# Pads that move TensorE's operands in SBUF, and another order of the first loads and splits

## The chip, the cores and the metric

The kernel runs on one core of one Trainium2 chip. The metric is device time in microseconds of one execution; the time of the kernel before is the median of three runs.

## The reference, cut

One sequence of 256 tokens with 1024 channels goes through two layers of a first block and one layer of a second block, all in fp32. Weights are used once for all 256 tokens, so most of the work is reading some 290 MB of weights and multiplying them with a small activation matrix.

```python
def first_block(x, ...):                      # two layers l
    h = _rmsnorm(x, norm_mix[l])
    p = h @ w_in[l]                           # 1024 x 3328, split over four mixers:
    branches = (rwkv7, stick_breaking, retention, conformer_conv)
    merged = sum(sigmoid(h @ w_gate[l, i]) * (branches[i] @ w_branch[l, i]) for i in range(4))
    x = x + merged @ w_out[l]
    h = _rmsnorm(x, norm_ffn[l])
    if l % 2 == 0: x = x + (silu(h @ ffn_w1) * (h @ ffn_w3)) @ ffn_w2      # width 2816
    else:          x = x + moe(h)             # top 2 of 8 SwiGLU experts, width 1408
def second_block(x, ...):                     # one layer
    proj = rms_norm(x) @ w_in                 # NSA attention, RG-LRU, two gates
    x = x + (sigmoid(ga) * (y_a @ w_proj_a) + sigmoid(gb) * (y_b @ w_proj_b)) @ w_out
```

## The kernel before, in words

**Products in three parts.** Every weight matrix is streamed from HBM in pieces of up to 128 x 2048 fp32 (tile `raw`, 1 MB, a DMA on SP's queue, `wload_` line 299). `wsplit_` cuts each half of a piece in a high part `wh` (ScalarE cast, line 266) and a rest `wl` (VectorE subtraction, line 267), both fp32r, 128 x 1024. Activations are split likewise, into `hh` and `hl` for the normed input, `uh`/`ul` inside the dense FFN, `bh`/`bl` for a mixer's branch, `mh`/`ml` for the merged sum, `xg` for the tokens gathered for an expert, `mu` for an expert's inner activations. A product is then three fp32r matmuls, all issued from line 131: in `dense`,

```python
if kind == "T":
    ps = ((h[:, kk, off:off + n], ah), (h[:, kk, off:off + n], al), (o[:, kk, off:off + n], ah))
else:
    x0, x1 = ah[:, j * P:(j + 1) * P], al[:, j * P:(j + 1) * P]
    ps = ((x0, h[:, kk, off:off + n]), (x0, o[:, kk, off:off + n]), (x1, h[:, kk, off:off + n]))
```

Kind "T" (nearly all) holds 128 columns of a weight stationary and streams 256 tokens of the activation. The other kinds hold the activation stationary and stream 384 or 512 columns of a weight: all w1, w3 and w2 products of the experts, and some projections ("R").

**Places in SBUF.** A tile's byte offset in each partition comes from the order in which pools and tiles are made. Pool `wp` has three slots each for `wh`, `wl` and `raw`. During the dense FFN and the experts, two more split slots stand in the pools `ffn` and `moe` (`spare`), and the slots are taken in turn. Tags `acth` and `actl` of pool `acts` (its tiles are `hh`/`hl`, later `mh`/`ml` of the second block and `hr` of the experts) lie right behind `wp`.

**Order.** A stage's work is written as generators, and a scheduler puts the instructions of each engine in order; `PLACES` pins some of TensorE's small products (recurrences, norms) between streamed ones. In one layer's mixers a chain of VectorE work (the RWKV-7 recurrence, near 110 to 180 us and 600 to 660 us) runs beside streamed products.

**The start** (`first_norm`, lines 1701 to 1731). SP loads constants, four pieces of `x` (tile `gth`), three pieces of `w_in`, the constants `c_mix` and small vectors (`pcvr`, `pcdr`); GpSimd's queue loads `wa`, `g2` and three vectors broadcast to all partitions (lines 530 to 538). ScalarE squares the four pieces of `x`, VectorE scales them by the inverse norm (line 1719), TensorE transposes them, and ScalarE (line 1728) and VectorE (line 1729) write `hh` and `hl` column block by column block. The list `behind` makes the first split wait for the scaled `x`. After the first 96 streamed products TensorE transposes the plain `x` again, for the residual `xT` (ScalarE copies, line 1742).

Of the kernel before, what the change touches and what calls it, by code (L numbers as in the profile page):

```python
# [18 lines left out]
P = 128  # L19
# [89 lines left out]
def build(tc, I, out, dbg=None, upto=99):  # L109
# [54 lines left out]
    ctile = {}  # L164
    late = {}

# [86 lines left out]
    def wsplit_(raw, k, n, perm):  # L253
        h, o = slot("split", [("wh", [P, 1024], F32R), ("wl", [P, 1024], F32R)])
        h = h[:, :k * n].rearrange("p (k n) -> p k n", n=n)
        o = o[:, :k * n].rearrange("p (k n) -> p k n", n=n)
        if perm:
            for g in range(2):
                src = raw[:, :, g * 256:(g + 1) * 256].rearrange("p k (b d) -> p k b d", d=64)
                hv = h.rearrange("p k (b g d) -> p k g b d", g=2, d=64)[:, :, g]  # L260
                ov = o.rearrange("p k (b g d) -> p k g b d", g=2, d=64)[:, :, g]
                for kk in range(k):
                    S.copy(out=hv[:, kk], in_=src[:, kk])
                    V.tensor_sub(out=ov[:, kk], in0=src[:, kk], in1=hv[:, kk])
        else:
            a = S.copy(out=h, in_=raw)  # L266
            i = V.tensor_sub(out=o, in0=raw, in1=h)  # L267
            if lead["n"]:
                lead["n"] -= 1
                if lead["late"] and not lead["n"]:  # L270
                    tc.add_manual_dep(i.ins, lead["late"].ins.name, nosync, reason="choice first")
                for x, y in zip((a, i), lead["ops"]):
                    tc.add_manual_dep(x.ins, y.ins.name, nosync, reason="activations first")
                for r in lead["hold"]:
                    tc.add_manual_dep(r.ins, i.ins.name, nosync, reason="first half first")
                lead["hold"] = ()
            if behind:
                tc.add_manual_dep(i.ins, behind.pop().ins.name, nosync, reason="norm first")
        return h, o

    def wload(src, k, n, rows=False, pinned=False):
        with tc.high_priority(offset=HP[1]):
            return wload_(src, k, n, rows, pinned)

    def wload_(src, k, n, rows, pinned):
# [9 lines left out]
        elif rows:  # L295
            for g in range(2):
                dma(out=r[g * 64:(g + 1) * 64], in_=src.rearrange("(g b p) n -> g p b n", g=2, p=64)[g])
        else:
# [194 lines left out]
    def bc_rows(mp, src, n, nm):  # L493
        t_ = mp.tile([P, n], F32, name=nm)
        nc.gpsimd.dma_start(out=t_, in_=bass.AP(tensor=src.tensor, offset=src.offset, ap=[[0, P], [1, n]]))
# [19 lines left out]
    def mix_layer(l):  # L515
        with ExitStack() as ls_:
# [10 lines left out]
            cload("c_mix", mp, nc.sync if l == 0 else nc.gpsimd)  # L527

            wa = mp.tile([P, 256], F32, name="wa")
            nc.gpsimd.dma_start(out=wa[0:64], in_=I["rw_w2"][l])  # L530
            nc.gpsimd.dma_start(out=wa[64:128], in_=I["rw_a2"][l])
            g2 = mp.tile([P, 256], F32, name="g2")
            nc.gpsimd.dma_start(out=g2, in_=I["rw_g2"][l])
            lnw = bc_rows(mp, I["rw_ln_w"][l], 256, "lnw")
            lnb = bc_rows(mp, I["rw_ln_b"][l], 256, "lnb")
            gn = bc_rows(mp, I["ret_gn"][l], 256, "gn")
            omu = mp.tile([P, 8], F32, name="omu")
            pts = [t2(f"pt{q}") for q in range(4)]
            for g in (1, 0):
# [8 lines left out]
                if g == 1:  # L548
                    if l == 0:
                        start_rest(mp)  # L550
                    V.tensor_scalar(omu, pc("mu"), -1.0, 1.0, op0=OP.mult, op1=OP.add)
                for c in range(4):
# [3 lines left out]
                    V.scalar_tensor_tensor(pt[:, b % 2, 1:], aps[c][:, :T - 1], pc("mu")[:, b:b + 1], pt[:, b % 2, 1:], op0=OP.mult, op1=OP.add)  # L556
            rT, kT, vT, pw = pts
# [757 lines left out]
    def lru(np_, W, hact):  # L1315
# [30 lines left out]
        V.scalar_tensor_tensor(ri, ri, 1.0, uc, op0=OP.add, op1=OP.mult)  # L1346
        a2 = np_.tile([P, 4, T], F32, name="la2", tag="lu")
# [96 lines left out]
    def moe(gain):  # L1444
        with ExitStack() as fs:
# [9 lines left out]

            xg = fp.tile([P, 2, KC, 2, P], F32R, name="xg")
# [5 lines left out]
            msq = [fp.tile([P, 2, T], F32, name="msq", tag="mth", bufs=3) for _ in range(3)]  # L1462
            mu = fp.tile([P, 2, 11, P], F32R, name="mu")
            hr = [ap_.tile([P, 2, D], F32R, name=f"hr{x}", tag=t_, bufs=1) for x, t_ in enumerate(("acth", "actl"))]
# [235 lines left out]
    def first_norm(mg, mp):  # L1700
# [3 lines left out]
        for j in range(2):  # L1704
            for a in range(2):
# [3 lines left out]
        start["pre"] = {1: [wload(I["w_in"][0, k * P:(k + 4) * P, 512:1024], 4, 512) for k in (0, 4)],  # L1709
                        0: [wload(I["w_in"][0, 0:512, 0:512], 4, 512)]}  # L1710
        xs = mp.tile([P, 2, 2], F32, name="xs")
        for j in range(2):
            for a in range(2):
                S.activation(out=h_rows[j][a], in_=x_rows[j][a], func=AF.Square, accum_out=xs[:, a, j:j + 1])
# [5 lines left out]
        behind.append(i)  # L1720
        start["gains"] = turned_columns(grows)
        hh, hl = ap_.tile([P, KC, T], F32R, name="hh", tag="acth", bufs=1), ap_.tile([P, KC, T], F32R, name="hl", tag="actl", bufs=1)
        for q in range(4):
            ps = rows_turned(h_rows, q)
            for c in range(2):
                k = 2 * q + c
                gk, pv = gains("nm", 0, 2)[:, k:k + 1], ps[:, c * T:(c + 1) * T]
                S.activation(out=hh[:, k], in_=pv, func=AF.Copy, scale=gk)  # L1728
                V.scalar_tensor_tensor(hl[:, k], pv, gk, hh[:, k], op0=OP.mult, op1=OP.subtract)
# [129 lines left out]
```

## Time and profile before

| | |
|---|---|
| time, median of 3 runs | 1436.39 us (1435.27 to 1437.26) |
| the profiled execution | 1438.56 us, of which the span is 1436.8 us |
| TensorE busy | 1382.1 us (96%), 10953 matmuls |
| VectorE busy | 1079.3 us (75%) |
| ScalarE busy | 804.5 us (56%) |
| mean granted clock of TensorE | 0.987 of full speed |
| HBM | 204 GB/s over the span |

A matmul's end is modelled in the profile, and successive matmuls overlap there. What one matmul adds to the time is the distance from its start to the next start, not its listed duration.

### The profile page before, as it was taken

How to read it: one execution, taken by the hardware profiler on the slowest of the kernel's cores; microseconds unless marked ns; L12 is line 12 of the kernel's file. 1: busy time of each engine (PE TensorE's matmuls, PEld its weight loads, DVE VectorE, ACT ScalarE, POOL GpSimd, SP SyncE). 2: the span in 40 equal slices, each digit the busy share in tenths (PEclk: the TensorE clock that was granted, in tenths of full speed). 3: DMA queues.
4: the chain of work that ended last, by engine and by line, in shares of the span. 5: the costliest groups of instructions: out<-in, count | busy, mean ns of one | idle time of the engine just before them, and what ended most of it. 6: DMA issues, size and time to landing. Idle time of an engine off the chain costs nothing. (4 is left out here: it accounts for less than half of the span.)

```text
span 1436.8 us, 26493 instructions
## 1 busy us (share of the span) xinstructions
PE 1382.1 (96%) x10953; PEld 1279.8 (89%) x10953; DVE 1079.3 (75%) x1569; ACT 804.5 (56%) x1126; POOL 54.7 (4%) x71
## 2 busy tenths in 40 slices
PE   5999999999999899998999799999999999899998
PEld 5999989999999889998999688888888888898997
DVE  4759966685655675797586799898898998767765
ACT  4643264564444454323544588788788777474643
POOL 1000010001000100002000000000000002010000
PEclk9999999999999999999999899999999999999999
DMA  7453134585566435422358599899799896734342
GB/s 242 150 193 118 32 120 162 187 296 189 194 131 209 137 128 169 147 87 75 132 183 293 187 365 355 296 361 356 282 371 358 287 339 207 262 120 131 107 134 101
DMA packets 137586, 294.24 MB, mean 205 GB/s; under 512 B 6949, under 2 KB 28845, under 8 KB 137200
## 3 DMA queue, kind: packets, MB, share of 16 engines
q1 hardware_dynamic: 133952, 282.48, 56.9%
q0 software_dynamic: 3424, 9.97, 2.9%
q8 instruction: 87, 1.43, 0.4%
q14 instruction: 43, 0.35, 0.1%
q10 hardware_dynamic: 80, 0.02, 0.0%
HBM read 289.82 MB, written 2.62 MB: 204 GB/s over the span
## 5 line engine op out<-in xcount | busy, mean ns | idle before, releaser
L267 DVE TENSOR_TENSOR wl<-raw,wh 128x1024 fp32r<-128x1024 f32 (+1 forms) x542 | 634.0, 1188 | 228.9 <-ACT wh L266 224.4
L266 ACT CAST wh<-raw 128x1024 fp32r<-128x1024 f32 (+1 forms) x542 | 549.1, 1022 | 444.5 <-PE mm L131 351.1
L131 PE MATMUL mm<-hh,wh 128*128 128x256 f32 x1376 | 396.7, 289 | 4.6 <-ACT hh L1728 3.0
L131 PE MATMUL mm<-hh,wl 128*128 128x256 f32 x1376 | 394.4, 287 | 5.0 <-DVE wl L267 2.5
L131 PE MATMUL mm<-hl,wh 128*128 128x256 f32 x1376 | 396.5, 288 | 0.0
L131 PEld LDWEIGHTS mm<-hh,wh 128*128 128x128 f32 x1376 | 267.3, 194 | 9.0 <-ACT hh L1728 3.4
L131 PEld LDWEIGHTS mm<-hh,wl 128*128 128x128 f32 x1376 | 267.1, 194 | 6.7 <-DVE wl L267 2.7
L131 PEld LDWEIGHTS mm<-hl,wh 128*128 128x128 f32 x1376 | 267.1, 194 | 3.5 <-issue 2.3
L131 PE MATMUL mm<-wh,xg 128*128 128x512 f32 (+1 forms) x768 | 231.5, 376 | 0.0
L131 PEld LDWEIGHTS mm<-wh,xg 128*128 128x128 f32 x768 | 142.7, 188 | 21.9
L131 PE MATMUL mm<-wl,xg 128*128 128x512 f32 (+1 forms) x384 | 143.9, 375 | 0.0
L131 PE MATMUL mx<-wh,mu 128*128 128x512 f32 x352 | 118.4, 398 | 0.0
L131 PEld LDWEIGHTS mm<-wl,xg 128*128 128x128 f32 x384 | 72.2, 188 | 11.2
L131 PEld LDWEIGHTS mx<-wh,mu 128*128 128x128 f32 x352 | 66.2, 188 | 13.5
L131 PE MATMUL mx<-wl,mu 128*128 128x512 f32 x176 | 69.3, 394 | 0.0
L955 DVE SCALAR_TENSOR_TENSOR cac<-cu,pcd,cac 128x256 f32<-128x256 f32 x120 | 52.9, 478 | 0.1
L131 PE MATMUL mx<-uh,wh 128*128 128x256 f32 x176 | 48.8, 280 | 1.4 <-ACT uh L218 1.4
L131 PE MATMUL mx<-ul,wh 128*128 128x256 f32 x176 | 49.1, 280 | 0.0
L131 PE MATMUL mx<-uh,wl 128*128 128x256 f32 x176 | 49.1, 279 | 0.0
L131 PE MATMUL mm<-nr,wh 128*128 128x256 f32 x192 | 38.3, 294 | 3.4 <-ACT nr L450 1.7
L131 PEld LDWEIGHTS mx<-wl,mu 128*128 128x128 f32 x176 | 33.1, 188 | 5.9
L131 PE MATMUL mm<-mh,wh 128*128 128x256 f32 x128 | 36.1, 282 | 0.0
(686 smaller groups left out, 2077.5 us busy)
## 6 DMA issues: line engine op xcount, KB each, us to landing
raw<-in_moe_w_dram SPq DMA_DIRECT2D x104, 1024.0 KB
raw<-in_w_in_dram SPq DMA_DIRECT2D x44, 1024.0 KB
raw<-in_ffn_w_dram SPq DMA_DIRECT2D x33, 1024.0 KB
raw<-in_w_gate_dram SPq DMA_DIRECT2D x32, 1024.0 KB
raw<-in_moe_w_dram SPq DMA_DIRECT2D x32, 768.0 KB
raw<-in_w_out_dram SPq DMA_DIRECT2D x12, 1024.0 KB
raw<-in_w_branch_dram SPq DMA_DIRECT2D x8, 1024.0 KB
raw<-in_moe_w_dram SPq DMA_DIRECT2D x8, 512.0 KB
```

The costliest lines, as they stand in the source:

```text
L131: i = getattr(nc.tensor, name)(*a, **k)
L266: a = S.copy(out=h, in_=raw)
L267: i = V.tensor_sub(out=o, in0=raw, in1=h)
L955: V.scalar_tensor_tensor(acc[:, b], cu[:, b, 2 + k:2 + k + T], dw[:, 2 * k + b:2 * k + b + 1], acc[:, b], op0=OP.mult, op1=OP.add)
```

## The change

**Pads.** A helper `pad(pool, n, name)` makes a tile of n bytes a partition that nothing uses, so that what follows in the pool stands n bytes further on. The byte offsets in the program as built, and what they leave when divided by 128 bytes:

| tile (pool) | before | after |
|---|---|---|
| `wh`, `wl` (wp) | 53184 to 73664 in steps of 4096: 64 | the same |
| `hh`, `hl` (acts) | 77760, 85952: 64 | 77824, 86016: 0 |
| `wh`, `wl` (ffn) | 120832 to 133120: 0 | 121344 to 133632: 0 |
| `uh`, `ul` (ffn) | 145408 to 159744: 0 | 145920 to 160256: 0 |
| `wh`, `wl` (moe) | 205888 to 218176: 64 | 207296 to 219584: 64 |
| `xg`, `mu` (moe) | 137216, 178432: 0 | 138176, 179648: 64 |
| `bh`, `bl`, `mh`, `ml` (mixers) | 64 in layer 0, 96 in layer 1 | 0, but for 16 of 768 products |

All offsets inside these tiles are multiples of 512 bytes. So of the streamed products of 256 columns, 3,768 with `hh` or `hl` and weights in `wp` go from (moving 64, stationary 64) to (0, 64); 360 with weights in the FFN's own two slots go from (64, 0) to (0, 0); 768 of the branches go to (0, 64). The experts' 1,680 wide products go from (64, 0) to (64, 64), and 192 products of 512 columns and 96 of 256 columns with `hh`, `hl`, `mh` or `ml` stationary go from (64, 64) to (64, 0). The 528 products of `uh` and `ul` stay (0, 64) or (0, 0).

**The start.** `x` is loaded and squared by channel halves; the two pieces of the first weight block are loaded in two halves each; the first three splits are tied to steps of the norm one after the other; `wa` moves from GpSimd's queue to SP's, behind the small vectors, and `c_mix`, `g2` and the broadcast vectors move to SP's queue behind the second weight block (layer 0 alone).

```diff
+    def pad(pool, n, nm):
+        pool.tile([P, n // 4], F32, name=nm, tag=nm, bufs=1)
...
             if behind:
-                tc.add_manual_dep(i.ins, behind.pop().ins.name, nosync, reason="norm first")
+                for x, y in zip((a, i), behind.pop(0)):
+                    tc.add_manual_dep(x.ins, y.ins.name, nosync, reason="norm first")
...
+        elif halves:
+            for x in range(2):
+                ks = slice(x * k // 2, (x + 1) * k // 2)
+                dma(out=r[:, ks], in_=src.rearrange("(k p) n -> p k n", p=P)[:, ks])
...
-            cload("c_mix", mp, nc.sync if l == 0 else nc.gpsimd)
             wa = mp.tile([P, 256], F32, name="wa")
-            nc.gpsimd.dma_start(out=wa[0:64], in_=I["rw_w2"][l])
-            nc.gpsimd.dma_start(out=wa[64:128], in_=I["rw_a2"][l])
             g2 = mp.tile([P, 256], F32, name="g2")
...
+            def first_vectors(eng):
+                eng.dma_start(out=wa[0:64], in_=I["rw_w2"][l])
+                eng.dma_start(out=wa[64:128], in_=I["rw_a2"][l])
+            def vectors(eng):
+                cload("c_mix", mp, eng)
+                eng.dma_start(out=g2, in_=I["rw_g2"][l])
+                return [bc_rows(mp, I[k][l], 256, nm, eng) for k, nm in (("rw_ln_w", "lnw"), ("rw_ln_b", "lnb"), ("ret_gn", "gn"))]
+            if l:
+                first_vectors(nc.gpsimd)
+                lnw, lnb, gn = vectors(nc.gpsimd)
...
+            pad(mp, (64, 32)[l], "padm")
...
                     if l == 0:
                         start_rest(mp)
+                        first_vectors(nc.sync)
...
+            if l == 0:
+                lnw, lnb, gn = vectors(nc.sync)
...
+        pad(np_, 64, "padl")
...
+            pad(fp, 448, "padx")
             xg = fp.tile([P, 2, KC, 2, P], F32R, name="xg")
...
+            pad(fp, 256, "padu")
             mu = fp.tile([P, 2, 11, P], F32R, name="mu")
+            pad(fp, 192, "pads")
...
-        for j in range(2):
-            for a in range(2):
+        for a in range(2):
+            for j in range(2):
                 nc.sync.dma_start(out=x_rows[j][a], in_=I["x"][0, j * P:(j + 1) * P, a * 512:(a + 1) * 512])
...
-        start["pre"] = {1: [wload(I["w_in"][0, k * P:(k + 4) * P, 512:1024], 4, 512) for k in (0, 4)],
+        start["pre"] = {1: [wload(I["w_in"][0, k * P:(k + 4) * P, 512:1024], 4, 512, halves=True) for k in (0, 4)],
                         0: [wload(I["w_in"][0, 0:512, 0:512], 4, 512)]}
...
-        behind.append(i)
+            if a == 0:
+                behind.append((sq, i))
         start["gains"] = turned_columns(grows)
+        pad(ap_, 64, "pada")
         hh, hl = ap_.tile([P, KC, T], F32R, name="hh", tag="acth", bufs=1), ap_.tile([P, KC, T], F32R, name="hl", tag="actl", bufs=1)
+        pad(ap_, 448, "padb")
...
+            if q in (0, 2):
+                behind.append((x, y))
```

ScalarE's queue at the start of the program, before the change: the squares of `x`, three casts of weights (`wh`), then the writing of `hh`.

```order
L1714 ACTIVATE gth,xs<-gth 128x512 x4
L266 CAST wh<-raw 128x1024 x3
L1728 ACTIVATE hh<-mx,pcg 128x256 x7
L266 CAST wh<-raw 128x1024
L1728 ACTIVATE hh<-mx,pcg 128x256
L266 CAST wh<-raw 128x1024 x2
L1742 COPY xT<-mx 128x512 x4
```

The same place after the change:

```order
L1738 ACTIVATE gth,xs<-gth 128x512 x4
L271 CAST wh<-raw 128x1024
L1755 ACTIVATE hh<-mx,pcg 128x256 x8
L1771 COPY xT<-mx 128x512
L271 CAST wh<-raw 128x1024 x3
L1771 COPY xT<-mx 128x512 x3
L271 CAST wh<-raw 128x1024 x3
```

Two casts have moved from ahead of `hh` to behind it, and a copy of the transposed `x` now stands ahead of the second cast. On TensorE the sixteen transposes for that copy have moved from behind the first 96 streamed products to behind the first 24.

SP's queue, which issues most DMAs, at the start before the change:

```order
L169 DMA c_id<-in_c_id_dram 128x256
L1706 DMA gth<-in_x_dram 128x512 x4
L299 DMA raw<-in_w_in_dram 128x4x512 x3
L169 DMA c_mix<-in_c_mix_dram 128x2192
L198 DMA pcvr<-in_rw_mu_dram 16x128
...
L198 DMA pcdr<-in_conv_dw_dram 124x128
L299 DMA raw<-in_w_in_dram 128x4x512 x3
```

And after it:

```order
L1730 DMA gth<-in_x_dram 128x512 x4
L307 DMA raw<-in_w_in_dram 128x2x512 x2
L309 DMA raw<-in_w_in_dram 128x4x512
L307 DMA raw<-in_w_in_dram 128x2x512 x2
L203 DMA pcvr<-in_rw_mu_dram 16x128
...
L542 DMA wa<-in_rw_w_dram 64x256
L543 DMA wa<-in_rw_a_dram 64x256
L309 DMA raw<-in_w_in_dram 128x4x512
L174 DMA c_mix<-in_c_mix_dram 128x2192
L547 DMA g_166<-in_rw_g_dram 128x256
```

The 1.1 MB of `c_mix` has moved from ahead of the small vectors to behind the fourth piece of weights, and `wa`, `g2` and the three broadcast vectors, which stood on GpSimd's queue, now stand here.

## Rows read from the trace of the kernel before

**Rows 1.** The page, busy time of each engine and its share of the span.

```profile
PE 1382.1 (96%) x10953; PEld 1279.8 (89%) x10953; DVE 1079.3 (75%) x1569; ACT 804.5 (56%) x1126; POOL 54.7 (4%) x71
```

**Rows 2.** Waits of the whole run: who for whom, us in total, times, longest.

```profile
ACT wh L266 <- PE mm L131: 351.1, 270, 12.7
...
PE mx L131 <- DVE g L1537: 8.4, 1, 8.4
```

**Rows 3.** TensorE's groups by shape, whole run: count, busy us, mean ns of one.

```profile
L131 PE MATMUL mm<-hh,wh 128*128 128x256 f32 x1376 | 396.7, 289 | 4.6 <-ACT hh L1728 3.0 <-ACT hh L218 1.6
...
L131 PE MATMUL mm<-wh,xg 128*128 128x512 f32 x512 | 164.1, 395 | 0.0
L131 PE MATMUL mx<-wh,mu 128*128 128x512 f32 x352 | 118.4, 398 | 0.0
L131 PE MATMUL mm<-wl,xg 128*128 128x512 f32 x256 | 100.8, 394 | 0.0
...
L131 PE MATMUL mm<-wh,xg 128*128 128x384 f32 x256 | 68.6, 339 | 0.0
L131 PE MATMUL mx<-ul,wh 128*128 128x256 f32 x176 | 49.1, 280 | 0.0
...
L131 PE MATMUL mm<-bh,wh 128*128 128x256 f32 x128 | 35.9, 284 | 0.0
```

**Rows 4.** The instructions in order of time, TensorE, 434 to 443 us: start, duration.

```profile
434.44 0.28 PE L131 MATMUL mm<-hh,wh 128*128 128x256 f32 x1
...
442.72 0.28 PE L131 MATMUL mm<-hh,wh 128*128 128x256 f32 x1
```

**Rows 5.** TensorE's groups by shape, 434.4 to 443.0 us.

```profile
L131 PE MATMUL mm<-hl,wh 128*128 128x256 f32 x25 | 7.1, 283 | 0.0
```

**Rows 6.** The same, 428.8 to 434.3 us.

```profile
L131 PE MATMUL mm<-hl,wh 128*128 128x256 f32 x17 | 4.8, 281 | 0.0
```

**Rows 7.** The same, 376.9 to 384.8 us.

```profile
L131 PE MATMUL mx<-ul,wh 128*128 128x256 f32 x24 | 6.6, 276 | 0.0
```

**Rows 8.** The same, 408.9 to 414.3 us.

```profile
L131 PE MATMUL mx<-uh,wh 128*128 128x256 f32 x16 | 4.5, 280 | 0.0
```

**Rows 9.** The same, 509.9 to 512.2 us.

```profile
L131 PE MATMUL mm<-nr,wh 128*128 128x256 f32 x14 | 2.5, 280 | 0.0
```

**Rows 10.** The same, 82.0 to 91.0 us.

```profile
L131 PE MATMUL mm<-wh,hl 128*128 128x512 f32 x14 | 5.4, 389 | 0.0
```

**Rows 11.** Stretch, its length; busy us of PE, PEld, DVE, ACT, POOL; PE clock; DMA share, GB/s.

```profile
120.00:170.00 50.00, 49.92 (x997) 46.58 (x996) 48.74 (x112) 13.99 (x21) 1.63 (x1) 1.00 0.27 87
...
940.00:980.00 40.00, 40.00 (x183) 33.14 (x182) 38.56 (x40) 32.80 (x37) 0.00 (x0) 1.00 1.02 374
```

**Rows 12.** TensorE in order of time, first 36 us: start, duration, idle before it.

```profile
12.63 3.86 PE L131 MATMUL mx<-c_id,gth 128*128 128x128 f32 x16 [6.05 <-DVE gth L1719]
19.54 0.79 PE L131 MATMUL mm<-hh,wh 128*128 128x256 f32 x2 [3.05 <-ACT hh L1728]
...
24.70 0.41 PE L131 MATMUL mm<-hh,wl 128*128 128x256 f32 x1
...
33.81 1.91 PE L131 MATMUL mx<-c_id,gth 128*128 128x128 f32 x16
```

**Rows 13.** ScalarE, the same stretch.

```profile
10.13 0.63 ACT L1714 ACTIVATE gth<-gth 128x512 f32<-128x512 f32 x1 [1.49 <-DMA gth<-in_x_dram]
...
15.34 1.99 ACT L266 CAST wh<-raw 128x1024 fp32r<-128x1024 f32 x2 [4.49 <-DMA raw<-in_w_in_dram]
...
19.02 2.66 ACT L1728 ACTIVATE hh<-mx,pcg 128x256 fp32r<-128x256 f32 x7
```

**Rows 14.** GpSimd, the same stretch: the DMAs that it issues.

```profile
1.25 0.72 POOL L530 DMA_DIRECT2D wa<-in_rw_w_dram  x1 [0.80 <-POOLq L1844]
...
4.12 0.56 POOL L495 DMA_DIRECT2D gn<-in_ret_gn_dram  x1
```

**Rows 15.** TensorE's groups by shape, 443.7 to 448.6 us.

```profile
L131 PE MATMUL mx<-uh,wh 128*128 128x256 f32 x15 | 4.2, 283 | 0.0
```

More of the change, by code (lines that the diff above doesn't have):

```diff
@@ L277, in wsplit_, with wload, wload_ @@
             if behind:
-                tc.add_manual_dep(i.ins, behind.pop().ins.name, nosync, reason="norm first")
+                for x, y in zip((a, i), behind.pop(0)):
+                    tc.add_manual_dep(x.ins, y.ins.name, nosync, reason="norm first")
         return h, o
-    def wload(src, k, n, rows=False, pinned=False):
+    def wload(src, k, n, rows=False, pinned=False, halves=False):
         with tc.high_priority(offset=HP[1]):
-            return wload_(src, k, n, rows, pinned)
-    def wload_(src, k, n, rows, pinned):
+            return wload_(src, k, n, rows, pinned, halves)
+    def wload_(src, k, n, rows, pinned, halves):
         raw, = slot("raw", [("raw", [P, 2048], F32)])
@@ L491, in ln_rows, with bc_rows @@
         V.tensor_tensor(out=y, in0=y, in1=r.unsqueeze(2).to_broadcast([P, 8, 64]), op=OP.mult)
-    def bc_rows(mp, src, n, nm):
+    def bc_rows(mp, src, n, nm, eng):
         t_ = mp.tile([P, n], F32, name=nm)
-        nc.gpsimd.dma_start(out=t_, in_=bass.AP(tensor=src.tensor, offset=src.offset, ap=[[0, P], [1, n]]))
+        eng.dma_start(out=t_, in_=bass.AP(tensor=src.tensor, offset=src.offset, ap=[[0, P], [1, n]]))
         return t_
@@ L525, in mix_layer @@
             hact = first_norm(mg, mp) if l == 0 else norm(gains("nm", l, 2), mg, "gth", 13)
-            cload("c_mix", mp, nc.sync if l == 0 else nc.gpsimd)
             wa = mp.tile([P, 256], F32, name="wa")
-            nc.gpsimd.dma_start(out=wa[0:64], in_=I["rw_w2"][l])
-            nc.gpsimd.dma_start(out=wa[64:128], in_=I["rw_a2"][l])
             g2 = mp.tile([P, 256], F32, name="g2")
[L533 to L536, printed above, removed]
+            def first_vectors(eng):
[8 more added lines that the diff above has]
+                lnw, lnb, gn = vectors(nc.gpsimd)
             omu = mp.tile([P, 8], F32, name="omu")
+            pad(mp, (64, 32)[l], "padm")
             pts = [t2(f"pt{q}") for q in range(4)]
@@ L1708, in first_norm @@
                                  ("ng", I["norm_gain_2"].rearrange("(a b) -> a b", b=P), 8)], "pcg", nc.scalar)
-        start["pre"] = {1: [wload(I["w_in"][0, k * P:(k + 4) * P, 512:1024], 4, 512) for k in (0, 4)],
+        start["pre"] = {1: [wload(I["w_in"][0, k * P:(k + 4) * P, 512:1024], 4, 512, halves=True) for k in (0, 4)],
                         0: [wload(I["w_in"][0, 0:512, 0:512], 4, 512)]}
         xs = mp.tile([P, 2, 2], F32, name="xs")
-        for j in range(2):
-            for a in range(2):
-                S.activation(out=h_rows[j][a], in_=x_rows[j][a], func=AF.Square, accum_out=xs[:, a, j:j + 1])
+        for a in range(2):
+            for j in range(2):
+                sq = S.activation(out=h_rows[j][a], in_=x_rows[j][a], func=AF.Square, accum_out=xs[:, a, j:j + 1])
         V.tensor_tensor(out=xs[:, 0], in0=xs[:, 0], in1=xs[:, 1], op=OP.add)
@@ L1727, in first_norm @@
                 gk, pv = gains("nm", 0, 2)[:, k:k + 1], ps[:, c * T:(c + 1) * T]
-                S.activation(out=hh[:, k], in_=pv, func=AF.Copy, scale=gk)
-                V.scalar_tensor_tensor(hl[:, k], pv, gk, hh[:, k], op0=OP.mult, op1=OP.subtract)
+                x = S.activation(out=hh[:, k], in_=pv, func=AF.Copy, scale=gk)
+                y = V.scalar_tensor_tensor(hl[:, k], pv, gk, hh[:, k], op0=OP.mult, op1=OP.subtract)
+            if q in (0, 2):
+                behind.append((x, y))
         start["x_rows"] = x_rows
```

## The prediction, made before the changed kernel had run

> **What bounds the kernel now.** I read the busy times first: TensorE is busy for 96% of the span, VectorE for 75% [rows 1]. Since a busy TensorE is not one at its peak, the list of waits comes next. ScalarE's casts of weights wait 351 us in 270 waits for matmuls to free a split slot, while TensorE's longest single wait is 8.4 us [rows 2]; casts, subtractions and DMAs all run ahead of TensorE. So the span is in the main the sum of the distances between matmul starts, and anything taken off those distances in the streamed stretches comes off the time, until VectorE gets in the way.
>
> How large is that distance? In a steady stretch of `hh`/`hl` products two rows 69 matmuls apart stand 8.28 us apart, 120 ns each [rows 4], and the same stretch lists 283 ns for one matmul [rows 5]. So a listed mean, less 163 ns, is the distance of steady matmuls; a mean over a whole run also holds some waits and cold stretches. Streaming 256 columns at 2.4 GHz, the level that the granted clock shows in nearly all of the span, is 106.7 ns of work: 13.3 ns are something else.
>
> The trace then shows that this rest depends on where the operands stand. Read by the moving and the stationary operand's offset modulo 128, at 256 columns:
> (64, 64): 283, so 120 ns [rows 5]; (64, 0), `hh` with weights in the FFN's slots: 281, so 118 [rows 6]; (0, 64), `uh`/`ul` with weights in `wp`: 276, so 113 [rows 7], but 280, so 117, in another such stretch [rows 8], and 280 for the (0, 64) tiles `nr` of a norm [rows 9].
> The whole-run mean for `ul` is 280 [rows 3]. With the 240 `uh`/`ul` products whose weights stand in the FFN's slots near 283, as at (64, 64), the 288 in `wp` come out near 277: most of these run at 113.
> At 512 columns the sign turns: (64, 64) has 389, so 226 [rows 10], the experts' (64, 0) have 394 to 398 [rows 3].
>
> So (0, 64) has two steady distances, 113 and 117 to 118. Which one a stretch falls in I can only read from what went before: the `uh` stretch at 113 follows products with weights in the FFN's own slots, those at 117 to 118 follow `hh` products at (64, 64) or a wait.
>
> **The change, part by part.**
> *Mixers and second block.* Of 3,768 `hh`/`hl` products that go to (0, 64), some 600 are in the dense FFN (its 1,056, less 96 on early `nr` tiles, less 360 in the FFN's slots), which leaves 3,168 in the mixers and the second block. Their stretches begin after small fp32 products and waits, as `nr` does. Bounds: 113 (7 ns each, 22 us) and 118 (2 ns each, 6.3 us). I take 118, nearest to `nr` [rows 9]: **-6.3 us**. Where VectorE is busy 48.7 of 50 us [rows 11] the gain is not TensorE's to keep, but only some 300 of these products lie in the two such stretches, 0.6 us.
> *Dense FFN.* Three of five split slots are in `wp`, two in the FFN's pool; after the change a (0, 64) stretch there follows a (0, 0) stretch, as the `uh` stretch of [rows 7] does. So I take 113 for the 600: 6.5 ns each, **-3.9 us** (bound at 118: -1.2). The 360 that become (0, 0) go from 118 to 120: **+0.7**.
> *Experts.* 1,296 products of 512 columns go from 394 to 398 [rows 3] to the 389 of [rows 10], 5 to 6 ns each once the waits in the 398 are left out: 6.8 us. For 384 of 384 columns no row shows the new place; between nothing and the 5 ns of the wider ones I take 1 ns, 0.4 us. VectorE is busy 38.56 of 40 us while experts stream [rows 11]; a TensorE that is 2.3% faster brings that to 39.4, just under. I count **-6.5 us**; if VectorE holds everything back there, 0.
> *Branches.* 768 products, 284 for `bh` [rows 3], to about 280 less the waits in it, 1 ns each: **-0.8** (bound at 113: -4).
> *What loses.* 192 products of 512 columns with the activation stationary go from (64, 64) to (64, 0), the experts' old case, 6 ns each: **+1.1**; 96 of 256 columns gain 0.2. The experts' gathers and scatters I leave at nothing: 128 products each way, a few ns.
> *The start.* The first streamed product starts at 19.54 us, after 3.05 us of waiting for `hh` [rows 12]. `hh` stands on ScalarE behind three casts, and the first of these waited for its 1 MB until 15.34 us [rows 13]. After the change one cast of a half piece stands there, so the wait is gone unless the transposes, which end at 16.49, come late: 3 us. The last piece of `x` lands at 10.1 us [rows 13], while GpSimd's DMAs, issued from 1.25 to 4.7 us [rows 14], load at the same time; they hold some 0.66 MB by their shapes. With `x` and the first piece, 1 MB each, that makes 2.7 MB by 15.34 [rows 13], from about 3 us on an estimated 0.2 MB/us, so at most 3 us come off the norm and, since `x` was issued ahead of most of them, rather none. The 213 ns spacing of the first 24 products or so (they end near 24.9, where 120 ns begins [rows 12]; the lower level of the clock) may also end sooner, since TensorE no longer stops between transposes and products: up to 24 times 93 ns, 2.2 us. Against that, ScalarE's second cast now stands behind the copy of `x`, hence behind TensorE's first 24 products and four transposes, so that the next products wait for cast and subtraction, about 1 us; and sixteen transposes come at the colder clock, 3.86 us against the 1.91 of those at 33.81 [rows 12], 2 us. Bounds -6 and -1; I take **-4**. `c_mix` and `wa` arrive later, but are used only by the recurrence after two blocks of 96 products, 20 us on; SP's next weight pieces come after 0.13 MB of `wa` in place of 1.1 MB of `c_mix`, so nothing there is late.
> Sum: -6.3 + 0.6 - 3.9 + 0.7 - 6.5 - 0.8 + 1.1 - 0.2 - 4 = -19.3, or 1419.3 against the profiled execution's own 1438.56. That one stands 2.2 above the median of the runs; from the median, **1417 us**.
>
> A rule speaks against the pads. The Trainium skill (SBUF — State Buffer, section "SBUF: two separate sides") says that TensorE has ports of its own and waits for nobody there, and TensorE: Matmul & The Clock Gate ("Back-to-back issue gap") puts warm isolated products at N/2.4 + 2.5 ns whatever their address, 109 ns at 256 columns (an estimate from that page). By these only the start would move. The trace does not agree: 113, 118 and 120 in equal products [rows 5 to 8].
>
> **Rivals.**
> *113 everywhere.* The mixers' stretches lock at 113 as most of `uh` does: 3,168 times 4.5 ns more, -14, so 1403. For it: the 113 stretches last over 72 products without a break [rows 7]. Against: `nr` [rows 9]. Chance 0.18.
> *VectorE holds.* In the experts the 3.6% that it is idle is used up by jitter, and the FFN stays at 118: 6.5 and 2.7 are lost, 1426. For it: 38.56 of 40 us [rows 11]; against: ScalarE, which feeds it, waits for TensorE there. Chance 0.13.
> *Only the start.* Distances depend on something else that went along with the offsets in these stretches, such as the slot or the pool: 1432.4. The page's rule names this case. Against it: the same product of `uh` lists 276 with weights in `wp` [rows 7] and 283 with weights in the FFN's slots, at (0, 0) [rows 15]. Chance 0.06.
> *Slower.* At 512 columns operands 64 bytes apart cost more, not less [rows 3, 10]. If the long `hh` stretches behave so, 5 ns each on 3,768 products is +19 in place of the -10.2 on `hh`: 1446. It turns the sign of the whole from +3 ns each. Against: no 256-column row 64 bytes apart is above 281. Chance 0.04.
>
> **How the numbers follow.** The sum's case has 0.57, with a range of its own from 1411 to 1423. The rivals above take 0.41; 0.02 is left for the start gaining nothing either. A measurement of this kernel tells a change from none at about 0.2%, 2.9 us. Faster: 0.57 + 0.18 + 0.13 and most of 0.06, 0.93; same 0.03; slower 0.04. The range runs from the 113 rival to the VectorE one, with 2 to 3 us for the start: 1400 to 1428; it leaves out the last two rivals and the tails.
>
> **What would show it.** In the changed kernel, `hh`/`hl` products should list 280 in steady mixer stretches and 276 in the dense FFN after products in its own slots; the experts' wide products 389 to 390; `wh` with `hh` or `mh` stationary 394 to 396. The first streamed product should start between 15 and 17 us. VectorE should be busy for 97 to 99% while experts stream, without TensorE waiting for it. The prediction is wrong if steady `hh` products stay at 283, if TensorE begins to wait for `wl` in the experts, or if the distance in the mixers is 113 in most stretches.

## The result, and the profile after

The changed kernel takes 1419.97 us (median of four runs, 1418.68 to 1422.56) beside 1436.6 us for the kernel before: a ratio of 0.9886, with a 95% interval of 0.9874 to 0.9898. It is 16.6 us faster; the sum had 19.3, and 1419.97 lies inside its own range of 1411 to 1423. The profiled execution has a span of 1416.9 us, 19.9 less than the one profiled before. 3.3 us of that belong to the two executions and not to the change; the last experiment shows what differs from one execution to the next.

The page's line of busy times answers to [rows 1]: TensorE is still busy for 96% of a shorter span, and the other engines do what they did.

```profile
PE 1361.9 (96%) x10953; PEld 1262.1 (89%) x10953; DVE 1078.2 (76%) x1569; ACT 805.4 (57%) x1126; POOL 51.3 (4%) x65
```

TensorE's groups by shape over the whole run answer to [rows 3].

```profile
L131 PE MATMUL mm<-hh,wh 128*128 128x256 f32 x1376 | 391.1, 284 | 2.3 <-ACT hh L223 1.6 <-DVE pcv L213 0.4 <-ACT wh L271 0.3
...
L131 PE MATMUL mm<-wh,xg 128*128 128x512 f32 x512 | 162.2, 391 | 0.0
L131 PE MATMUL mx<-wh,mu 128*128 128x512 f32 x352 | 117.3, 394 | 0.0
L131 PE MATMUL mm<-wl,xg 128*128 128x512 f32 x256 | 99.8, 390 | 0.0
...
L131 PE MATMUL mm<-wh,xg 128*128 128x384 f32 x256 | 68.6, 338 | 0.0
L131 PE MATMUL mx<-ul,wh 128*128 128x256 f32 x176 | 49.4, 281 | 0.0
...
L131 PE MATMUL mm<-bh,wh 128*128 128x256 f32 x128 | 35.6, 281 | 0.2 <-DVE gth L1031 0.2
...
L131 PE MATMUL mm<-wh,hl 128*128 128x512 f32 x32 | 12.7, 395 | 0.0
```

The `hh` products list 284 in place of 289, the experts' 512-column products 390 to 394 in place of 394 to 398, the 384-column ones 338 in place of 339. `bh` went from 284 to 281. Two groups list more: `ul` (281 in place of 280) and `wh` with `hl` stationary (395, where [rows 10] has 389).

In steady stretches the same groups read as forecast: 279 to 280 for `hh` and `hl` in a mixer (212 to 222 us), where the starts stand 117.8 ns apart. In the branches of that layer (224 to 238 us) 276 is listed through 126 products.

```profile
L131 PE MATMUL mm<-hl,wh 128*128 128x256 f32 x29 | 8.1, 280 | 0.0
L131 PE MATMUL mm<-hh,wl 128*128 128x256 f32 x29 | 8.1, 279 | 0.0
```

```profile
L131 PE MATMUL mm<-bl,wh 128*128 128x256 f32 x42 | 11.6, 276 | 0.0
```

The first 21 us of TensorE in order of time answer to [rows 12]. Sixteen transposes start 2.4 us sooner, the first streamed product starts at 13.71 in place of 19.54, and the listed duration falls to 0.28 us at the fourth product, where before it stayed at 0.41 for the first 5 us. Then the transposes for `xT` come, and behind them two waits, 0.31 for a cast and 0.54 for a subtraction.

```profile
10.20 3.86 PE L131 MATMUL mx<-c_id,gth 128*128 128x128 f32 x16 [4.50 <-DVE gth L1743]
13.71 0.56 PE L131 MATMUL mm<-hh,wh 128*128 128x256 f32 x1
14.07 0.41 PE L131 MATMUL mm<-hl,wh 128*128 128x256 f32 x1
...
14.47 0.28 PE L131 MATMUL mm<-hh,wh 128*128 128x256 f32 x1
...
16.95 1.91 PE L131 MATMUL mx<-c_id,gth 128*128 128x128 f32 x16
19.17 0.39 PE L131 MATMUL mm<-hh,wh 128*128 128x256 f32 x1 [0.31 <-ACT wh L271]
...
20.43 0.38 PE L131 MATMUL mm<-hh,wl 128*128 128x256 f32 x1 [0.54 <-DVE wl L272]
```

ScalarE in the same stretch answers to [rows 13]: the last square of `x` starts at 7.72 in place of 10.13, one cast stands ahead of `hh`, and it waits 0.62 us for its half MB in place of 4.49 for a whole one.

```profile
7.72 0.63 ACT L1738 ACTIVATE gth<-gth 128x512 f32<-128x512 f32 x1
...
9.06 1.04 ACT L271 CAST wh<-raw 128x1024 fp32r<-128x1024 f32 x1 [0.62 <-DMA raw<-in_w_in_dram]
11.54 0.48 ACT L1755 ACTIVATE hh<-mx,pcg 128x256 fp32r<-128x256 f32 x1 [1.43 <-PE mx L131]
```

While experts stream (920 to 960 us, the columns of [rows 11]) VectorE is busy for 39.17 of 40 us, and TensorE never idles there.

```profile
920.00:960.00 40.00, 40.00 (x190) 33.96 (x189) 39.17 (x40) 33.82 (x38) 0.00 (x0) 1.00 1.03 379
```

### The profile page after: what moved, and what is told of

The parts are those of the page before. It is cut to its first block, busy times and chain, and to the rows that moved or that the text cites. A ratio compares the mean times of both kernels' runs of the same rounds, so it can differ in the third digit from the quotient of the medians.

```text
span 1416.9 us, 26493 instructions
## 1 busy us (share of the span) xinstructions
PE 1361.9 (96%) x10953; PEld 1262.1 (89%) x10953; DVE 1078.2 (76%) x1569; ACT 805.4 (57%) x1126; POOL 51.3 (4%) x65
## 5 line engine op out<-in xcount | busy, mean ns | idle before, releaser
L131 PE MATMUL mm<-hh,wl 128*128 128x256 f32 x1376 | 388.0, 282 | 5.6 <-DVE wl L272 3.1
L131 PE MATMUL mm<-hh,wh 128*128 128x256 f32 x1376 | 391.1, 284 | 2.3 <-ACT hh L223 1.6
L131 PE MATMUL mm<-hl,wh 128*128 128x256 f32 x1376 | 389.9, 283 | 0.2 <-DVE hl L224 0.2
L131 PEld LDWEIGHTS mm<-hh,wl 128*128 128x128 f32 x1376 | 260.7, 190 | 7.5 <-DVE wl L272 3.5
L131 PEld LDWEIGHTS mm<-hh,wh 128*128 128x128 f32 x1376 | 261.0, 190 | 6.7 <-issue 2.7
L131 PEld LDWEIGHTS mm<-hl,wh 128*128 128x128 f32 x1376 | 260.8, 190 | 3.4 <-issue 1.8
L131 PE MATMUL mx<-wh,mu 128*128 128x512 f32 x352 | 117.3, 394 | 0.0
L131 PE MATMUL mm<-bh,wh 128*128 128x256 f32 x128 | 35.6, 281 | 0.2 <-DVE gth L1031 0.2
```

What stands on the lines that cost most here:

```text
L131: i = getattr(nc.tensor, name)(*a, **k)
```

## The experiments

All times are medians in us; a ratio is to runs of the kernel before on the same chip, whose median was 1436.3 to 1436.8 in every set.

**The parts by themselves: `e1_pads` and `e2_start`.** `e1_pads` is the kernel before with every `pad(...)` line of the diff, `e2_start` the changed kernel with this edit:

```diff
     def pad(pool, n, nm):
-        pool.tile([P, n // 4], F32, name=nm, tag=nm, bufs=1)
+        return
```

> All pads of the change with the first loads and splits in the old order. Theory (the offsets of the two operands set the distance of matmuls): the products of hh and hl in the mixers list 279 to 280 ns as in the changed kernel, the experts' wide ones 389; the first streamed product still starts near 19.5 us; the time is the 1436.6 of before less the 10 to 13 us that the stages behind the start gained, 1424 to 1427. Rival (the distance hangs on something that went along with the offsets, only the start gained): 283 and 394 to 398 stay, 1435 to 1438.

> The new order of the first loads and splits without any pad. Theory: the first streamed product starts near 13.7 us, the lead over before is about 6 us by the end of the first 240 streamed products and stays there; hh lists 283 in steady stretches, the experts' wide products 394 to 398; 1430 to 1431. Rival (the lead of the start is given back at the recurrence, whose constants now come later): 1434 to 1437.

Measured: pads alone 1425.39 (0.9924, 0.9903 to 0.9944), the start alone 1430.12 (0.9962, 0.9949 to 0.9976). The gains, 10.9 and 6.2, add up to 17.1, next to the 16.6 of both. In a mixer the `hh` products list 279 with the pads (218 to 228 us) and 283 without (215 to 225 us), and the first streamed product starts at 19.37 and at 14.40. Only the rows of the part that was kept moved. In the trace of `e2_start` the lead over before is 4.9 us at the 240th streamed product, where about 6 was expected, and still 5.0 past the first layer's recurrence, so the rival of a lead given back falls.

```profile
L131 PE MATMUL mm<-hh,wl 128*128 128x256 f32 x29 | 8.1, 279 | 0.0
```

```profile
L131 PE MATMUL mm<-hh,wl 128*128 128x256 f32 x28 | 7.9, 283 | 0.0
```

So the rival "only the start" falls: with the old start the pads still take three quarters of a per cent.

**The expert stage: `e3_acts`**, the changed kernel without three lines:

```diff
-            pad(fp, 448, "padx")
-            pad(fp, 256, "padu")
-            pad(fp, 192, "pads")
```

> The changed kernel without the three pads of the expert stage, so that xg and mu stand at 0 again. Theory: the experts' 512-column products list 394 to 398 again and the stage is 5 us longer; 1424 to 1426. Rival (VectorE sets the pace of the expert stage, so its pads give nothing): 1419 to 1421.

Measured: 1425.5 (0.993, 0.9912 to 0.9947), 5.5 us over the changed kernel. The experts' products are back at [rows 3]'s 395 (whole run), so these three pads are worth about a third of the gain, and VectorE did not hold them back.

```profile
L131 PE MATMUL mm<-wh,xg 128*128 128x512 f32 x512 | 164.1, 395 | 0.0
```

**The distances by themselves: `e4_places`.** A program of its own: one tile at each offset, stretches of 24 to 72 products, most of them behind a wait of TensorE for VectorE.

```python
OFFS = (0, 32, 64, 96)
m = {o: place(o, f"m{o}") for o in OFFS + (128, 192, 256, 320, 384, 448)}
s = {o: place(o, f"s{o}") for o in OFFS + (448,)}
...
for mo in OFFS:
    for so in OFFS:
        after_gap(mo, so, N)
```

> None of the reference's work: stretches of fp32r products from tiles at chosen offsets, by themselves, the output is a constant block. Theory: after a wait, 256 columns at (moving 0, stationary 0) and (64, 64) stand 120 ns apart, (64, 0) and (0, 64) 117 to 118; straight behind a (0, 0) stretch (0, 64) stands at 113, straight behind (64, 64) at 118; at 512 columns equal offsets give 226 to 227 and (64, 0) 231 to 233; only the offset modulo 128 counts, so that 0, 128, 256 and 384 against a stationary at 448 are alike. Rival (slot, pool or the traffic of other engines decides): all sixteen pairs of offsets are alike while nothing else runs, and they part only where ScalarE and VectorE run beside them.

Measured, from the starts in the trace, ns from one product to the next (mean of a stretch without its first products; pairs are moving, stationary):

| moving and stationary offset | 256 columns | 512 columns |
|---|---|---|
| the same: (0, 0), (32, 32), (64, 64), (96, 96) | 120 in each | 227 in each |
| 64 apart: (0, 64), (64, 0), (32, 96), (96, 32) | 113.3 or 118, each stretch at one of them | 233, 229, 233, 229 |
| 32 apart either way (eight pairs) | 117 to 120, uneven from product to product | 233 to 234 |
| moving 0, 128, 256, 384, stationary 448 | 118 in each | not run |
| moving 192, 448, stationary 448 | 120 in each | not run |
| moving 64, 320, stationary 448 | 119, uneven | not run |

The grouped rows of three stretches, (0, 0), (0, 64) and (64, 0), read 283, 276 and 279:

```profile
L74 PE MATMUL gp<-m,s 128*128 128x256 f32 x44 | 5.4, 283 | 0.0
```

```profile
L74 PE MATMUL gp<-m,s 128*128 128x256 f32 x39 | 4.6, 276 | 0.0
```

```profile
L74 PE MATMUL gp<-m,s 128*128 128x256 f32 x33 | 4.0, 279 | 0.0
```

The pairs part while no other engine runs, and with ScalarE casting beside them (0, 0) and (0, 64) gave the same 120 and 113. VectorE's subtractions, meant for the same stretches, ran before 40 us, beside the first (0, 0) stretch (120 too), so their traffic beside (0, 64) is not tested here. The rival is gone but for that. Two parts of the expectation failed. Equal offsets modulo 128 are alike only where they are equal modulo 256 too (the last two lines). In the kernel the equal pairs are, but pairs 64 apart modulo 128 come in two kinds there: modulo 256 the slots of `wp` stand at 192, the expert pool's at 64 before the change, and the FFN's own at 64 in the runs from `e6_slots` on. And a stretch at (0, 64) straight behind (0, 0) stood at 118 here, one behind (64, 64) at 113, and 113 also appeared at (64, 0): which of the two a stretch gets is not told by the class of the stretch ahead of it.

**What picks 113 or 118: `e5_lock` and `e7_entry`.** Again programs of their own, with the stationary operand at 0 and the moving one shifted inside its tile:

```python
x = TE.matmul(w[:, :cols], wts[:, so // 4 + k * P:so // 4 + (k + 1) * P],
              area[:, mo // 4 + c * 256:mo // 4 + c * 256 + cols], ...)
```

> None of the reference's work: the stationary operand at 0, the moving one from 0 to 120 in steps of 8 bytes, each twice behind a wait; then stretches at (0, 64) broken by single products of other widths or offsets. Theory (the moving operand and the next stationary one are read side by side and meet in the same place when their offsets agree): 120 near 0 and near 128, the least distance near a difference of 64, 113 or 118 there by how the stretch began, and some of the breaks turn a stretch at 118 into one at 113 or back while others never do. Rival (only whole steps of 64 matter): all differences between 8 and 56 are like 0, and a break changes nothing.

Measured: a break does decide. Behind single products of 32 to 160 or 240 columns a stretch at (0, 64) came out now at 113, now at 118; behind one of 248 all four stood at 118; behind one of 192 or 224 columns all eight stretches stayed at 113, behind one at (0, 0) all four stayed at 118. Behind one at a moving offset of 16, 32 or 96 all stood at 113, behind one at 80 at 118. At other differences the distance was 117 to 122 without an order that I could read (8: 117 and 120; 56: 119 and 120; 88: 120), so "least near 64" is too simple; and at a difference of 112 both stretches settled at 113 to 114.

> None of the reference's work: ten entries each, behind a wait, into stretches with the moving operand at 64, 104, 108, 112, 116 and 120 and the stationary one at 0; then thirty stretches at (0, 64), in each a single product with the moving operand at 16, 32 or 96 in the middle. Theory (which of the two distances a stretch gets is chance at its entry, and a later disturbance can draw it again): at a difference of 64 both 113 and 118 appear among the ten; at 112, where both stretches so far ended at 113, all ten do; a product at 32 turns stretches at 118 into 113 more often than back. Rival (113 at 112 was chance too): entries at 112 are spread as at 64.

Measured: at 112 the ten entries begin at 117 to 120, and every one long enough to tell (the six of 16 products or more) runs into 113.3; 104 and 108 stay at 120, 116 and 120 at 120 to 122. At (64, 0) all ten stood at 118, which neither theory had; of the thirty entries at (0, 64), 22 stood at 113. A product at 16 in the middle turned three of four stretches from 118 to 113 and none back, one at 32 none of two, one at 96 one of two. The last stretch at a difference of 112, from its tenth product on, and the last one at (64, 0):

```profile
L42 PE MATMUL gp<-mv,st 128*128 128x256 f32 x11 | 1.4, 275 | 0.0
```

```profile
L42 PE MATMUL gp<-mv,st 128*128 128x256 f32 x10 | 1.3, 279 | 0.0
```

**No slot at the activations' offset: `e6_slots`**, the changed kernel with

```diff
                 hact = norm(gains("nf", l, 2), fp, "fth", 12, halves=True)
+                pad(fp, 64, "padf")
...
+                        if g0 == 0 and c == 0:
+                            pad(fp, 448, "padg")
                         uh = fp.tile([P, 2, T], F32R, name="uh", tag="uh", bufs=4)
```

> The changed kernel with the dense FFN's own two split slots moved from 0 to 64, by a pad of 64 bytes ahead of them and one of 448 ahead of the inner activations, so that all hh, hl, uh and ul products there are at (0, 64). Theory: the 600 products that were at (0, 0) go from 120 to 118, 1.2 us, and to 113 where a stretch starts so, 4 us; 1416 to 1419. Rival (the 113 of the kernel before came from the change between the slots' offsets, so that without it all stay at 118): 1419 to 1420, no stretch at 113.

Measured: 1415.88 (0.9862, 0.9838 to 0.9886). In the dense FFN 831 of 952 `hh`/`hl` products stand at 113 (counted here and below: products that another of the same shape follows without a wait), and the stage is 5.7 us shorter than in the changed kernel's first trace; the rival falls. Beside the second trace of the changed kernel (`after_again`) it is 4.7 us shorter, 1.5 of them the lower clock. The interval still touches that of the changed kernel.

**The offset that settles: `e8_48` and `e9_best`.** `e8_48` builds on `e6_slots`:

```diff
+    def shifted(nm, tag, off=48):
+        t_ = ap_.tile([P, KC * T + 128], F32R, name=nm, tag=tag, bufs=1)
+        return t_[:, off // 4:off // 4 + KC * T].rearrange("p (k t) -> p k t", t=T)
...
-        hh = ap_.tile([P, KC, T], F32R, name="hh", tag="acth", bufs=1)
-        hl = ap_.tile([P, KC, T], F32R, name="hl", tag="actl", bufs=1)
+        hh, hl = shifted("hh", "acth"), shifted("hl", "actl")
```

and `e9_best` does the same for `uh` and `ul`, and puts the second block's `mh` and `ml` at 64.

> The kernel of e6_slots with hh and hl 48 bytes further on, so that they stand 112 bytes (modulo 128) from every weight of a split slot. Theory (at a difference of 112 every entry finds its way to 113 after some ten products, at 64 the entry decides): the hh and hl products of both mixers and the second block, some 2,900 steady ones, go from 117 to 118 to 113, 10 to 12 us; 1403 to 1407. Rival (the convergence holds only with the stationary operand at 0, as measured, or not beside other engines' traffic): 117 to 119 stay, 1415 to 1420.

> As e8_48, and also the dense FFN's inner activations uh and ul at 48 and the second block's merged sum mh and ml at 64 in place of 0. Theory: uh and ul list 276 in all stretches, 0.5 us; 96 products of 512 columns go from 233 to 227, 0.6 us; 1 us below e8_48, which the runs may not tell apart. Rival (a change between tiles at 48 and tiles at 0 costs nothing and locks as well): the same as e8_48 but for 0.6 us.

Measured: `e8_48` 1416.09 (0.9854, 0.9838 to 0.987), `e9_best` 1418.04 (0.9877, 0.9854 to 0.9899). In the mixers and the second block the distances did what the theory said. In `e8_48` 807 of 955 `hh`/`hl` products of the first mixer layer (without the first 240) stand at 113, in the second layer 862 of 1,058, in the second block 603 of 713; in the changed kernel it was 106 of 955, 21 of 1,075 and 3 of 695. A mixer stretch lists 275 (212 to 222 us), where the changed kernel has 279 to 280:

```profile
L131 PE MATMUL mm<-hl,wh 128*128 128x256 f32 x30 | 8.2, 275 | 0.0
```

In the dense FFN and for `mh`/`ml` they did not, and the modulus is why: `hh` at 48 stands 112 bytes from the slots of `wp` (192 modulo 256), but 240 from the FFN's own (64). With `wp` 496 of 597 products stand at 113, with the FFN's own slots 59 of 339, at a mean of 117.2 ns. `uh` and `ul` at 48 in `e9_best` part in the same way, 114.3 and 117.2. And its products of 512 columns with `mh` and `ml` at 64, weights at 192, took 232.3 ns, not 227.

The time did not follow: some 8.7 us less in these distances than in `e6_slots`' trace outside the FFN, and the same median. The profiled execution of `e8_48` took 1419.97 us, the longest of its four, that of `e6_slots` 1412.64, the shortest of its four. Of that difference the dense FFN has 4.5 us: 1.6 with `uh` at 0 beside `hh` at 48 (nearly all its stretches at 118), 1.4 with `hh` at the FFN's own slots, 1.5 at the lower clock. The second block has 2.7, of which 1.7 are the lower clock, below. The two mixer layers, which should have gained 3.1 and 3.9, came out 0.6 shorter and 0.8 longer. TensorE's longest waits show one place there, the recurrence's solving step of both layers, where `e6_slots` has no such wait:

```profile
PE mx L131 <- DVE sc L660: 3.0, 2, 1.5
```

VectorE is at its limit in that stretch [rows 11], so what TensorE saves ahead of it is waited out there. But about half of the 1.5 us has another source: VectorE comes to that step 0.7 us later than in `e6_slots`, because ahead of it it waits 1.5 us for a power that GpSimd computes, in place of 0.4. That power took 2.63 us in both layers of `e8_48`, `e9_best` and `e10_pins`, and 1.63 or 1.64 in the eight other traces of the kernel, here `e6_slots` and `e8_48`:

```profile
115.34 1.63 POOL L385 TENSOR_TENSOR tlis<-tlis,smallc 128x8 f32<-128x8 f32 x1 [66.88 <-DVE tlis L384]
```

```profile
115.08 2.63 POOL L389 TENSOR_TENSOR tlis<-tlis,smallc 128x8 f32<-128x8 f32 x1 [66.63 <-DVE tlis L388]
```

In the three with 2.63 us VectorE's next subtraction of a weight starts 0.08 to 0.09 us ahead of the power, in the others 0.02 to 0.09 behind it. That this order is the cause fits all 22 cases, but no run changes it alone. Still, the interval of `e8_48` lies just under those of both sets of the changed kernel, and no version here was clearly faster than `e8_48` and `e6_slots`. `e9_best`, expected 1 us below `e8_48`, is 2 above with an interval that overlaps; at the FFN's entry its trace has a wait of 2.3 us for a subtraction that `e8_48` has not.

**Undoing that wait: `e10_pins`**, `e9_best` with

```diff
-("solve", 753), ("turn", 764)
+("solve", 768), ("turn", 779)
```

> As e9_best, with TensorE's small products of the recurrence's solving step placed behind 768 and 779 streamed products of a mixer layer in place of 753 and 764. Theory (where hh stands at 113 TensorE comes to that step before VectorE is done, and the two waits of 1.5 us there give part of the gain back): the two waits near 127 and 602 us go or shrink below 0.5 us each, 2 to 3 us; 1412 to 1417. Rival (VectorE sets the pace of the whole recurrence, so the wait only moves to the next step, the states): waits of the same sum behind it, 1416 to 1420.

Measured: 1424.18 (0.9905, 0.9883 to 0.9928), above what either theory has, though its six executions run from 1420.08 to 1427.98 and its interval overlaps that of `e9_best`. The two waits, 3.0 us in `e9_best` too, grew:

```profile
PE mx L131 <- DVE sc L660: 5.1, 2, 2.5
```

So TensorE is not merely early: the product with the mask that it waits for (`sc`) stands on VectorE behind work that moves ahead of it when the step is placed later, in the first layer four steps of a convolution and a weight's subtraction, 2.7 us. How to place the step for the faster products stays open.

**GpSimd's loads at the start: `e11_pool`**, the changed kernel with

```diff
-            if l:
-                first_vectors(nc.gpsimd)
-                lnw, lnb, gn = vectors(nc.gpsimd)
+            first_vectors(nc.gpsimd)
+            lnw, lnb, gn = vectors(nc.gpsimd)
```

and `c_mix` alone loaded where `vectors(nc.sync)` stood.

> The changed kernel with wa, g2 and the three broadcast vectors of layer 0 back on GpSimd's queue at the start of the program; c_mix stays where the change put it. Its scheduler also puts the transposes for xT later, behind the streamed products as in the kernel before. Theory (those 0.66 MB share the DMA engines with the pieces of x): the last square of x ends 1 to 2.5 us later than the 7.7 to 8.3 us of the changed kernel, the first streamed product starts at 15 to 16 us, and the time is 1421 to 1423. Rival (the order of the pieces alone brings x forward): squares end by 8.4, the first streamed product starts near 13.7, 1419 to 1421.

Measured: 1420.85 (0.9887, 0.9869 to 0.9904). The last square starts at 9.20 and the first streamed product at 15.21, 1.5 us later on either count, as the theory has it. At the 241st streamed product it is 1.7 to 2.4 us behind the two traces of the changed kernel; the times, 1420.85 beside 1419.97 and 1421.55, do not tell them apart, and lie in the rival's range.

```profile
9.20 0.63 ACT L1737 ACTIVATE gth<-gth 128x512 f32<-128x512 f32 x1 [0.35 <-DMA gth<-in_x_dram]
```

```profile
15.21 0.46 PE L131 MATMUL mm<-hh,wh 128*128 128x256 f32 x1
```

**The changed kernel once more: `after_again`.**

> The changed kernel itself on the same chip, for the comparison with the others: 1419 to 1421, its mixers' hh products at 117 to 118 with some stretches at 113; which stretches these are may differ from the run before.

Measured: 1421.55 (0.9893, 0.9877 to 0.991). Its trace and that of the first execution have the same program and two differences. One is which of the two distances a stretch got. Of the first products 167 of 223 stood at 113 in the first trace, 17 of 225 here. In the dense FFN it was 168 of 597 `hh`/`hl` products at (0, 64) in the first trace and 504 here; `e1_pads`, `e3_acts` and `e11_pool`, alike in this stage, had 504, 432 and 504. The same stretch reads 280 in the first (379.6 to 385 us) and 276 in the second (382 to 388 us):

```profile
L131 PE MATMUL mm<-hl,wh 128*128 128x256 f32 x15 | 4.2, 280 | 0.0
```

```profile
L131 PE MATMUL mm<-hl,wh 128*128 128x256 f32 x16 | 4.4, 276 | 0.0
```

The other is the granted clock. On entering the FFN TensorE waits 1.58 us for `hh` in both executions. In the first the clock stayed at 1.00 behind it; in the second it fell, to a mean of 0.79 over 8 us, and 33 matmuls ran in a stretch where 47 did (the columns of [rows 11]).

```profile
302.40:310.40 8.00, 5.98 (x47) 5.58 (x48) 8.00 (x16) 5.38 (x8) 0.00 (x0) 1.00 0.99 368
```

```profile
304.00:312.00 8.00, 5.97 (x33) 5.56 (x34) 8.00 (x16) 3.86 (x7) 0.00 (x0) 0.79 0.98 366
```

Counting the streamed products, and the experts' gathers, that list over 1.55 ns a column (the lower level) in each trace: 136 before, 71 after, 102 in `after_again`, 82 in `e6_slots`, 133 in `e8_48`, 145 in `e10_pins`. Each costs some 93 ns, and they come in runs of up to 27 behind waits of TensorE, not behind the same waits each time. From 71 to 136 is 6 us, of which the 24 at the start, where the changed kernel has 2, are the change's. This is why a profiled pair may differ from the medians by some us, and why waits of one or two microseconds can cost more than they last.

## Why the prediction was right, step by step

**The kernel is the sum of its distances.** Right in the main. Pads that leave TensorE's order of products as it was took 10.9 us (8.0 to 13.9 by the interval). But the sum's terms for them add up to 15.3: they were too large by 4.4, the start's term too small by 2.2, and that the total came within 3 us is in part the luck of two misses that offset each other. Between the same products of the traces of before and `e1_pads`, with 93 ns taken off for each product at the lower clock, the first mixer layer is 2.0 us shorter, the dense FFN 2.9, the second layer 2.1, the experts 4.9, the second block not at all.

**The start, -4.** Right in kind, too small: 6.2 by `e2_start` (3.4 to 7.3 by the interval; 4.9 at the 240th product of its trace). The first streamed product, forecast for 15 to 17 us, starts at 13.71. The wait for the first 1 MB is gone, and the lower clock ended at the fourth product, so most of the 2.2 us allowed for it came. The sum held "rather none" for GpSimd's loads; they held `x` up by 1.5 us (`e11_pool`). The price of the waits behind the second transposes, those for `xT`, 1 us, was 0.85. The 2 us put down for these transposes at the colder clock were not paid: they took 1.91 us in all, as before, since the clock had risen ahead of them.

**Mixers and second block, -6.3 at 118.** Right as a distance: 119.8 to 117.3 for the first layer's `hh`/`hl` products, 119.8 to 117.7 for the second's, 119.8 to 117.8 in the second block, and 119.9 to 114.5 for the 240 at the start: together 7.8 on 3,168. The time kept less. With the branches and the losses below, the terms add up to -5.6 in these stages, and by the stages of `e1_pads` above it was 4.0, none of it in the second block; TensorE's idle time there grew by 2.2 us. So the 0.6 us set against the gain was too little: a shorter distance is not all TensorE's to keep where its next products wait for another engine's results. In the first trace of the changed kernel the second block was even 1.5 us longer than before, 1.3 of it the lower clock, which came once more at 1281 us.

**Dense FFN, -3.9 + 0.7.** Four of five traces have it, nearly: in `after_again` 114.3 to 111.6 us for the 960 `hh`/`hl` products and 61.7 to 61.4 for the 528 of `uh`/`ul`. The trace of the changed kernel shown above is the fifth, with 113.1 and 62.4. The reason given, that a stretch behind (0, 0) takes 113, is not a rule: `e4_places` has it at 118. So the size came out, and its reason did not; that is luck. What a stretch gets is settled where it is entered or disturbed, and it is then kept, through stretches at (0, 0) too.

**Experts, -6.5.** Mis-sized by a quarter (its own parts, 6.8 and 0.4, add up to 7.2): the distance fell from 231.5 to 227.1 ns for the 768 products of 512 columns with `xg` and from 232 to 228.7 for the 528 with `mu`, 5.1 us together; the stage is 4.9 shorter, and `e3_acts` gives 5.5. The mean of 394 to 398 hid two kinds. With weights in the slots of `wp` (192 modulo 256) the products stood 233 ns apart before the change, with those in the expert pool's own slots (64) 229.5, as (0, 64) and (64, 0) do in `e4_places`. So two products of five had 2.4 ns to gain and not 5 to 6. The 384-column products, priced at 1 ns, gained nothing (174.2 and 174.3). VectorE at 97.9% held nothing back, so that rival falls.

**Branches and losses.** The branches and merged sums gained 1.8 us of distance in place of 0.8, since two runs, of 142 and 111 products, stood at 113. The 192 wide products with the activation stationary lost 1.2, forecast 1.1.

Of the rivals, "113 everywhere" needs places that this kernel does not have; and where `e8_48` brings most of it about, the time is 1416, not 1403. *Slower* is refuted by the `hh` rows, 280 in place of 283. The Trainium skill's gap for isolated products (TensorE: Matmul & The Clock Gate, "Back-to-back issue gap") would be 109 ns at 256 columns, an estimate from that page; no steady stretch here shows less than 113.3, and what it leaves out, the operands' places, is the 2 to 7 ns that this change is about.

What stays open: why the offsets matter. In `e4_places` nearly every weight load starts 2 to 4 ns behind the matmul that runs beside it, so the two reads overlap, but that they meet in the memory is argued from that, not shown. Nor is it known what makes a stretch at (0, 64) enter at 113 or at 118.

## What to carry to other kernels

Where a matmul-bound kernel streams 256 or 512 columns per weight load, read the distance between starts against the offsets of both operands, modulo 256 bytes and not 128. Equal offsets cost 120 ns at 256 columns, where other places had 113 to 122, and were the best at 512; at 384 columns the change made no difference. A pad in a pool costs no instruction and tests it. Price a gain per stage: here TensorE's extra speed was kept in the dense FFN and the experts, where ScalarE's casts waited for it, and waited out in part in the mixers and the second block, where TensorE's small products wait for VectorE.

## What the runs showed of the hardware that was not expected

The same stretch of the same program has two steady distances, 113.3 and 118 ns, and keeps the one it entered with for 70 products and more, over a change of tiles as well. At a difference of 112 bytes, entries that begin at 117 to 120 find their way to 113.3 within some ten products, in the program of its own and in the kernel's mixers; at 240 bytes (48 and 64), the same modulo 128, they did not (59 of 339). And the granted clock falls behind some waits of 1 to 3 us in one execution and not in the next, at 93 ns for each 256-column product until it is back.
